# Seven heads' queries and keys and one head's forget gates as four pairs of seven block products ahead of the attention

## The chip, the cores and the metric

One core of one Trainium2 chip runs the whole kernel. TensorE (PE in the profile) multiplies, VectorE (DVE), ScalarE (ACT) and GpSimd (POOL) do the rest, SyncE (SP) issues DMAs, and so do ACT and POOL. The metric is the device time of one execution in microseconds; lower is better.

## The reference

One encoder layer on 1024 tokens of width 1024. The input is RMS-normalised and multiplied by one wide weight matrix; its columns are queries, keys and values of an attention with 8 heads of 64, then forget gates `f`, values `i`, queries `q` and output gates `g` of a gated recurrence (HGRN2) with 4 heads of 128, then two merge gates.

```python
xn = rmsnorm(x, norm1_g[layer])
u = xn @ w_in[layer].astype(f32)
c = np.cumsum([SB_WIDTH, SB_WIDTH, SB_WIDTH, HG_WIDTH, HG_WIDTH, HG_WIDTH, HG_WIDTH, D_MODEL])
q_sb, k_sb, v_sb, f_raw, i_hg, q_hg, g_hg, gate_sb, gate_hg = jnp.split(u, list(c), axis=-1)
...
z = jnp.einsum('bhqd,bhkd->bhqk', qi, k) * scale
mask = kpos[None, :] < qpos[:, None]
log_beta = jax.nn.log_sigmoid(z)
log_rem = jnp.where(mask, log_beta - z, 0.0)
between = lax.cumsum(log_rem, axis=3, reverse=True) - log_rem
w = jnp.where(mask, jnp.exp(log_beta + between), 0.0)
return jnp.einsum('bhqk,bhkd->bhqd', w, v)
...
h = x.astype(f32) + merged @ w_out[layer].astype(f32)
hn = rmsnorm(h, norm2_g[layer])
a = jnp.square(jax.nn.relu(hn @ w_ff1[layer].astype(f32)))
h = h + a @ w_ff2[layer].astype(f32)
```

The two branches are gated and merged, projected, added to the input, and a squared-ReLU MLP and a last RMSNorm follow.

## The kernel before

**Numbers in two parts.** Every matmul operand is split into a high part (ACT copies to the rounded type, `hi_copy`) and a low part (DVE subtracts, `lo_sub`); `hi_lo` does both, and `three` multiplies high by high, high by low and low by high. A block of 128 output columns, 512 tokens and 512 inputs is 12 matmuls of 512 columns.

**Stages.** First x is loaded, normalised and transposed into `xn` (two halves of 512 tokens, each as high and low slots), while head 0's queries and keys (`qk0`) and the first four heads' values (`v0`) are projected. Then comes the attention, then the recurrence (`hg_levels`, `hg_tail`) with the merge gates' products as filling, then the merge, the output projection and the MLP. The merge gates, the output projection and the MLP already use sums of blocks, with seven block products in place of eight.

**Attention.** `items` holds 8 heads times 8 query blocks in the order 7, 0, 6, 1, 5, 2, 4, 3. For each item `scores` (L774 on) multiplies the query block with the keys and lets ACT take the sigmoid into `rm`; `weights` runs the products from right to left as one scan on DVE (L821; two scans for block 7); `turn` transposes the result on PE, ACT subtracts one into `wTh` (L869) and DVE makes `wTl` (L875); `values` multiplies two finished blocks with V, and ACT and DVE add the halves of the result (L903, L904). The loop issues the scores of item i+2, the scan of item i+1 and the turn of item i.

**Order.** A planner orders instructions at compile time by their place in the program and their readiness; on PE two lanes are held in order by hand: "main" (the attention) and "fill" (projections), where a fill block waits for the main block two before it. `Stream` holds fill jobs; each call of `step` issues one piece (six matmuls of 512 columns, or twelve of 256). When a job starts, its weights are split, and `prefetch` splits those of the next job and loads those of the one after. All loads on SP's queue keep the program's order (`load`).

**What fills the attention.** The stream `st` holds qk0 with v0, qk1 to qk3, v1 (the other four heads' values), qk4 to qk7, then f0, q0, i0, g0 of the recurrence, f1, q1, g1 and then raw job 0 of the merge gates. The loop issues 126 steps over 64 items, so that everything up to g0 is done in the attention. `qk_epilogue` writes the keys' high and low parts into one slot (KS, high in partitions 0 to 63, low in 64 to 127) and the queries' into two (QH, QL), and POOL copies each query part into the other 64 partitions by a DMA.

**Storage.** 40 slots of 128 x 1024 floats and 10 halves of 128 x 512 hold nearly all data; raw weights and their two parts have two buffers each (`wpool`).

Of the kernel before, what the change touches and what calls it, by code (L numbers as in the profile page):

```python
# [9 lines left out]
F32 = mybir.dt.float32  # L10
# [29 lines left out]
def kernel(  # L40
# [493 lines left out]
    st = Stream()  # L534
# [158 lines left out]
    def qk_epilogue(h):  # L693
        def ep(ps, half):
            if half == 0:
                qk[h] = tuple(slot(f"{n}{h}", F32R) for n in ("QH", "QL", "KS"))
            QH, QL, KS = qk[h]
            cs = slice(half * 512, (half + 1) * 512)
# [12 lines left out]
    def v_job(quad):  # L711
        unit = v_unit(quad)
        return st.add(
            [unit], lambda: token_steps(f"pjv{quad}", unit, xn, range(NT), v_epilogue(quad))
        )

    def qk_item(h):
        u = cols_unit(f"wqk{h}", [(W_IN, C_Q + h * DHS, DHS), (W_IN, C_K + h * DHS, DHS)])
        return f"pjqk{h}", u, qk_epilogue(h)
# [24 lines left out]
    def first_job():  # L744
# [4 lines left out]
        def body():  # L749
            v_ep = v_epilogue(0)  # L750
            for half, parts in enumerate((((0, 2), (2, 2)), ((0, 4),))):
                ps = bank(f"{name}_{half}")
                for b0, n in parts:
# [4 lines left out]
                    if half == 0 and b0 > 0:  # L758
                        st.prefetch()
# [3 lines left out]
        return st.add([u_qk], body), u_qk, u_v  # L763

    j_first, u_qk0, u_v0 = first_job()
    j_qk = {0: j_first}
    for h in range(1, NHS):
        j_qk[h] = proj_jobs([qk_item(h)], xn)
        if h == 3:
            j_v = v_job(1)  # L770
# [144 lines left out]
    def hg_slot(h, key, half):  # L915
        if half == 0:
# [52 lines left out]

    def hg_jobs(h):  # L970
        for key, c0, ep in (
            ("f", C_F, f_epilogue(h)),
            ("q", C_QH, silu_epilogue(h, "q")),
            ("g", C_GH, silu_epilogue(h, "g")),
        ):
            if key == "g" and h % 2 == 0:
                i_job(h)
            u = cols_unit(f"w{key}{h}", [(W_IN, c0 + h * P, P)])
            j_hg[h] = proj_jobs([(f"pj{key}{h}", u, ep)], xn)

    hg_jobs(0)
# [442 lines left out]

    j_raw = []
    hg_jobs(1)
    j_raw.append(raw_job(0))
    hg_jobs(2)
    j_raw.append(raw_job(1))
    j_raw.append(raw_job(2))  # L1430
    hg_jobs(3)
# [723 lines left out]
    st.advance(4, 1)  # L2155
    u_v0.split()
    norm1((2, 3))
    st.advance(3, 1)
    norm_transpose(xn, 0, 2, 2)
    st.advance(5, 1)  # L2160
    norm1(range(4, NT))
    st.advance(4, 1)
# [4 lines left out]
    st.advance(11, j_qk[0])  # L2167
    first_row()
# [169 lines left out]
```

## Time and profile before

| | |
|---|---|
| median of 3 runs | 1459.29 us (1457.73 to 1460.15) |
| profiled execution | 1460.9 us, span 1458.7 us |
| start to first score | 0 to 50.3 us |
| attention, first score to last value matmul | 50.3 to 322.3 us |
| recurrence and its filling | 322.3 to about 700 us |

The span is the time between the first and last instruction that the profiler saw. A row of stretches gives, after the stretch and its length, each engine's busy time with the number of instructions, then the granted share of the TensorE clock, the DMA engines' busy share and GB/s. A group's row gives line, engine, operation, destination and sources, shapes and count, then busy time, mean ns of one, idle time before it and what ended it. A timeline row gives start and length in us. A row of waits gives total, times and longest, in us.

### The profile page before, as it was taken

To read this page: it belongs to the slowest core of one execution; us is meant where nothing else is said; L and a number is where in the kernel's file an instruction comes from. 1 tells how busy PE (TensorE), PEld (TensorE's weight loads), DVE (VectorE), ACT (ScalarE), POOL (GpSimd) and SP (SyncE) were. 2 spreads that over 40 slices of the span, in tenths; PEclk is the share of its full clock that TensorE was granted. 3 is DMA by queue.
4 is the path that set the end of the run, shared out by engine and by line. 5 is a ranking of instruction groups with operands and counts; after the bars stand their busy time and mean duration, and the time that the engine had idled before them with its cause. 6 is when DMAs were issued, how large, how long until landed. Compare 5 with 4: busy or idle time off the path is not lost. (4 is left out here: it accounts for less than half of the span.)

```text
span 1458.7 us, 19714 instructions
## 1 busy us (share of the span) xinstructions
PE 1438.6 (99%) x7470; PEld 1224.4 (84%) x7470; DVE 1060.9 (73%) x1498; ACT 645.8 (44%) x1068; POOL 164.1 (11%) x306
## 2 busy tenths in 40 slices
PE   9999999999999999999998999999999999999998
PEld 8889888988898888888877888888888888888886
DVE  6576788679747688877756898666666757768765
ACT  7454565542313234433344575444444533523433
POOL 4222232200000012100010210000000000000032
PEclk9999999999999999999999999999999999999999
DMA  7344364311313249655478513444445975676835
GB/s 227 88 120 102 83 117 98 74 36 44 94 30 101 63 133 246 228 176 180 139 211 291 186 62 133 171 152 152 159 159 171 347 266 196 240 275 244 284 103 182
DMA packets 159862, 232.00 MB, mean 159 GB/s; under 512 B 26092, under 2 KB 94232, under 8 KB 159768
## 3 DMA queue, kind: packets, MB, share of 16 engines
q1 hardware_dynamic: 142552, 183.29, 37.4%
q0 software_dynamic: 13472, 40.91, 11.2%
q10 hardware_dynamic: 3744, 6.56, 1.2%
q8 instruction: 59, 0.97, 0.3%
q14 instruction: 35, 0.29, 0.1%
HBM read 166.75 MB, written 63.97 MB: 158 GB/s over the span
## 5 line engine op out<-in xcount | busy, mean ns | idle before, releaser
L821 DVE TENSOR_TENSOR_SCAN rm<-rm,bits 128x512 f32<-128x512 f32 (+6 forms) x72 | 87.2, 1222 | 27.3 <-ACT rm L795 26.9
L154 ACT CAST whid<-w 128x1024 fp32r<-128x1024 f32 x30 | 31.6, 1053 | 154.4 <-PE pm L131 83.7
L131 PE MATMUL pm<-wlod,sh 128*128 128x512 f32 x240 | 93.5, 390 | 0.0
L131 PE MATMUL pm<-whid,sl 128*128 128x512 f32 x240 | 93.4, 389 | 0.0
L131 PE MATMUL pm<-whid,sh 128*128 128x512 f32 x240 | 93.4, 389 | 0.0
L131 PE MATMUL pm<-tl,sh 128*128 128x512 f32 (+1 forms) x210 | 81.3, 387 | 0.0
L131 PE MATMUL pm<-th,sh 128*128 128x512 f32 (+1 forms) x210 | 81.3, 387 | 0.0
L131 PE MATMUL pm<-th,sl 128*128 128x512 f32 (+1 forms) x210 | 81.3, 387 | 0.0
L875 DVE SCALAR_TENSOR_TENSOR wTl<-pw,wTh 128x512 fp32r<-128x512 f32 (+2 forms) x96 | 50.6, 549 | 38.8 <-ACT wTh L869 38.5
L159 DVE TENSOR_TENSOR wlod<-w,whid 128x1024 fp32r<-128x1024 f32 x30 | 36.7, 1222 | 57.0 <-ACT whid L154 57.0
L869 ACT ACTIVATE wTh<-pw,minus_one 128x512 fp32r<-128x512 f32 (+2 forms) x96 | 53.1, 581 | 45.0 <-PE pw L134 43.4
L159 DVE TENSOR_TENSOR sl<-sa,sh 128x1024 fp32r<-128x1024 f32 x56 | 68.1, 1217 | 0.5 <-ACT sh L154 0.5
L1979 POOL TENSOR_SCALAR fss<-fss 128x1 f32<-128x1 f32 x8 | 4.5, 562 | 562.5 <-ACT fsc L1974 562.0
L154 ACT CAST sh<-sa 128x1024 fp32r<-128x1024 f32 x56 | 57.2, 1046 | 6.2 <-DMA sa<-ad 6.2
L131 PEld LDWEIGHTS pm<-wlod,sh 128*128 128x128 f32 x240 | 45.0, 187 | 9.9 <-DVE wlod L159 0.4
L131 PEld LDWEIGHTS pm<-whid,sl 128*128 128x128 f32 x240 | 45.1, 188 | 9.4
L131 PEld LDWEIGHTS pm<-whid,sh 128*128 128x128 f32 x240 | 45.1, 188 | 9.2
L131 PE MATMUL pX<-sql,t1h 128*128 128x512 f32 x128 | 50.1, 391 | 0.1
L131 PE MATMUL pX<-sqh,t1h 128*128 128x512 f32 x128 | 49.9, 390 | 0.1
L131 PE MATMUL pX<-sqh,t1l 128*128 128x512 f32 x128 | 49.8, 389 | 0.0
L795 ACT ACTIVATE rm<-z 128x512 f32<-128x512 f32 (+3 forms) x96 | 43.6, 489 | 8.6 <-PE z L131 7.5
L131 PEld LDWEIGHTS pm<-tl,sh 128*128 128x128 f32 x210 | 39.5, 188 | 8.1
(929 smaller groups left out, 4546.9 us busy)
## 6 DMA issues: line engine op xcount, KB each, us to landing
w<-in_w_ff_dram SPq DMA_DIRECT2D x72, 512.0 KB, 5.4
sa<-ad SPq DMA_DIRECT2D x56, 512.0 KB, 6.6
ad<-a SPq DMA_DIRECT2D x32, 256.0 KB, 4.1
ad<-s SPq DMA_DIRECT2D x16, 512.0 KB, 4.7
tw<-in_w_out_dram POOLq DMA_DIRECT2D x24, 256.0 KB, 4.7
x<-in_x_dram SPq DMA_DIRECT2D x8, 512.0 KB, 8.9
vr<-vrows POOLq DMA_DIRECT2D x16, 256.0 KB, 5.1
xnl<-xnh POOLq DMA_DIRECT2D x8, 512.0 KB, 9.9
```

Source lines behind the costliest of these rows:

```text
L131: return pe(nc.tensor.matmul(*a, **k))
L154: hi_last[0] = after(in_turn("act", nc.scalar.copy(dst, src)), hi_behind[0])
L159: nc.vector.tensor_tensor(out=dst, in0=src, in1=hi.bitcast(F32), op=ALU.subtract),
L795: nc.scalar.activation(rm[:, s0 : s0 + m], z[:, :m], AF.Sigmoid, scale=-0.125)
L821: sc = nc.vector.tensor_tensor_scan(out=rr, data0=rr, data1=bits[:, 1024 - nk + a : 1024 - nk + b][:, ::-1], initial=rm[:, b : b + 1] if i ...
L869: nc.scalar.activation(th[:, 0:n, qs], src, AF.Identity, bias=minus_one),
L875: nc.vector.scalar_tensor_tensor(out=tl[:, 0:n, qs], in0=src, scalar=-1.0, in1=th[:, 0:n, qs].bitcast(F32), op0=ALU.add, op1=ALU.subtract,),
L1979: nc.gpsimd.tensor_scalar(out=ssq, in0=ssq, scalar1=1.0 / D, scalar2=EPS, op0=ALU.mult, op1=ALU.add)
```

## The change

The projections of q and k for heads 1 to 7 and of f0 leave the stream. They become eight blocks of 128 columns in four pairs, (qk1, qk2), (qk3, qk4), (qk5, qk6), (qk7, f0), and each pair is computed ahead of the attention as seven block products (`ProjPair`) in place of eight: both column blocks, both halves of the tokens and both halves of the 1024 inputs give a two by two block product.

- `early_whole` adds the high and low parts of `xn` back together, the first half on POOL, the second on DVE; `early_sums` makes four sums of blocks from them and splits each into two parts. Products 3, 5, 6 and 7 use these, products 1, 2 and 4 use `xn` itself.
- Each pair loads two raw weight blocks, splits the first as it is (`split_plain`, products 1 and 2) and forms sums and differences of both (`split_sums`, products 3 to 7).
- Products 1, 6, 7 and 4 accumulate in bank X with copies by ACT in between; 5 and 3 in Y; 2 in Z; DVE adds the copies (`value`).
- Queries and keys are no longer kept: `qk_store` splits each half and writes both parts to DRAM (POOL's queue), also for head 0; `qk_load` reads a head back by six loads on SP's queue into KS, QH and QL.
- A second stream `front` holds qk0 with v0, and v1. Eight steps of v1 run before the pairs, three in the last pair, two between the first two scores, the rest in the attention.
- `st` now begins with raw job 0 and q0, i0, g0; the loop issues 45 steps over 64 items. In item 2 of a head the next head's q and k are read, in item 3 its values (item 2 before), in item 5 its values are split.

```diff
-    def qk_epilogue(h):
-        def ep(ps, half):
-            if half == 0:
-                qk[h] = tuple(slot(f"{n}{h}", F32R) for n in ("QH", "QL", "KS"))
...
-            hi_copy(KS[0:64, cs], ps[64:128])
-            hi_copy(QH[0:64, cs], ps[0:64])
-            lo_sub(KS[64:128, cs], ps[64:128], KS[0:64, cs])
-            last_lo[0] = lo_sub(QL[0:64, cs], ps[0:64], QH[0:64, cs])
-            for Q in (QH, QL):
-                nc.gpsimd.dma_start(Q[64:128, cs].bitcast(F32), Q[0:64, cs].bitcast(F32))
+    def qk_store(h):
+        def ep(src, half_):
+            cs = slice(half_ * 512, (half_ + 1) * 512)
+            hi, lo = half(f"qkh{h}_{half_}", F32R), half(f"qkl{h}_{half_}", F32R)
+            last_lo[0] = hi_lo(hi, lo, src)
+            for n, t in (("h", hi), ("l", lo)):
+                nc.gpsimd.dma_start(qkd[h, n][:, cs], t.bitcast(F32))
...
+    def qk_load(h):
+        qk[h] = QH, QL, KS = tuple(slot(f"{n}{h}", F32R) for n in ("QH", "QL", "KS"))
+        hi, lo = qkd[h, "h"], qkd[h, "l"]
+        q, k = slice(0, DHS), slice(DHS, P)
+        for t, r, src in (
+            (KS, q, hi[k]), (QH, q, hi[q]), (KS, k, lo[k]), (QH, k, hi[q]), (QL, q, lo[q]),
+            (QL, k, lo[q]),
+        ):
+            load(t[r].bitcast(F32), src)
...
+    def early_whole(half_, engine):
+        for kp in range(KT // 2):
+            h, l = (t.bitcast(F32) for t in xn.t[half_, kp])
+            early[half_, kp // 2, kp % 2] = t = slot(f"xw{half_}{kp}")
+            engine.tensor_tensor(out=t, in0=h, in1=l, op=ALU.add)
...
+        for kp in range(2):
+            tt(w[1, 1, kp], w[1, 0, kp], w[1, 1, kp], ALU.add)
+            tt(w[1, 0, kp], w[0, 0, kp], w[1, 0, kp], ALU.subtract)
+            tt(w[0, 0, kp], w[1, 1, kp], w[0, 0, kp], ALU.subtract)
+            form(6, kp, w[0, 0, kp])
...
+        def split_plain(self):
+            hl = self.wts("a")
+            hi_lo(*hl, self.raw[0])
...
+        def split_sums(self):
...
+            sub_(ra[:, a], rb[:, a], ra[:, a])
+            sub_(rb[:, a], rb[:, b], rb[:, a])
+            self.w[3] = tuple(half(f"w3{n}{self.i}", F32R) for n in "hl")
+            hi_lo(*self.w[3], rb[:, b])
+            sub_(rb[:, b], rb[:, b], ra[:, a])
+            sub_(ra[:, b], ra[:, b], rb[:, b])
+            hl = self.wts("b")
+            hi_lo(*hl, rb)
+            self.w[7], self.w[6] = self.halves_of(hl)
+            hl = tuple(slot(f"w54{n}{self.i}", F32R) for n in "hl")
+            hi_lo(*hl, ra)
...
-    j_raw = []
-    hg_jobs(1)
-    j_raw.append(raw_job(0))
+    j_raw = [raw_job(0)]
+    hg_job(0, "q")
+    hg_job(0, "g")
...
+    early_whole(0, nc.gpsimd)
+    front.advance(4, 1)
     norm_transpose(xn, 1, 0, 4)
...
+    early_whole(1, nc.vector)
+    early_sums()
...
+    front.finish(j_first)
+    front.advance(8, j_v)
+    proj[0].load()
+    proj[0].split_plain()
+    proj[0].m1()
+    proj[0].split_sums()
+    for o, n in zip(proj, proj[1:] + [None]):
+        o.m2()
+        if n:
+            n.load()
+        o.m6()
+        o.m5()
+        if n:
+            n.split_plain()
+        o.m7()
+        if n:
+            n.m1()
+            n.split_sums()
+        else:
+            qk_load(0)
+            v_load(0)
+            front.advance(3, j_v)
+        o.m4()
+        o.m3()
...
-    n_fill = 9 * (j_hg[0] - j_qk[0]) + 18
-    n_first = 3
+    n_fill = 3 + 7 + 2 * 9 + 17
+    n_first = 0
...
-        if ahead < NHS and i % NHS in (2, 5):
+        if ahead < NHS and i % NHS in (2, 3, 5):
             if ahead == NHS // 2:
-                st.finish(j_v)
-            (v_load if i % NHS == 2 else v_split)(ahead)
+                front.finish(j_v)
+            {2: qk_load, 3: v_load, 5: v_split}[i % NHS](ahead)
...
-        upto = (j_hg[2], j_hg[3], j_raw[5], j_sb[1], j_sb[3])[h]
+        upto = (j_hg[2], j_hg[3], j_raw[6], j_sb[1], j_sb[3])[h]
```

More of the change, by code (lines that the diff above doesn't have):

```diff
@@ L758, in body @@
                     if half == 0 and b0 > 0:
-                        st.prefetch()
+                        front.prefetch()
                     tb = 4 * half + b0
                     yield from token_steps("pjv0", u_v, xn, range(tb, tb + n), v_ep, tb == 0)
-        return st.add([u_qk], body), u_qk, u_v
+        return front.add([u_qk], body), u_qk, u_v
     j_first, u_qk0, u_v0 = first_job()
[L766 to L770, printed above, removed]
+    j_v = v_job(1)
@@ L915, in hg_slot @@
     def hg_slot(h, key, half):
-        if half == 0:
+        if (h, key) not in hg:
             hg[h, key] = slot(f"{key}{h}")
```

158 lines of the change are left out of this document (127 added, 31 removed).

## The prediction

> **What bounds the kernel now.** I read the page first (share of each engine), then the stretches of the stage in question, then PE's waits, then single rows for prices.
>
> ```profile
> span 1458.7 us, 19714 instructions
> PE 1438.6 (99%) x7470; PEld 1224.4 (84%) x7470; DVE 1060.9 (73%) x1498; ACT 645.8 (44%) x1068; POOL 164.1 (11%) x306
> ```
>
> ```profile
> core 0: us, PE busy (x) PEld busy (x) DVE busy (x) ACT busy (x) POOL busy (x), PEclk, DMA share, GB/s
> 50.30:322.30 272.00, 267.85 (x1691) 239.78 (x1690) 197.28 (x268) 148.90 (x308) 66.17 (x146) 0.99 0.41 91
> 322.30:700.00 377.70, 377.70 (x2117) 322.53 (x2116) 292.46 (x521) 127.56 (x243) 34.45 (x50) 1.00 0.42 129
> ```
>
> ```profile
> PE po L131 <- DVE wTl L875: 3.0, 3, 1.6
> PE po L131 <- ACT wTh L869: 0.6, 1, 0.6
> PE z L131 <- ACT rm L795: 0.5, 1, 0.5
> ```
>
> PE is busy in 99% of the span. That share alone says little, as matmuls overlap; but the waits of PE in the attention (first score matmul at 50.3 us, last value matmul at 322.3) come to 4.1 us of 272.0. So TensorE sets the pace there and in the 377.7 us of the recurrence behind it. DVE has 197.28 us of 272.0, 73%. The reader should keep both: matmuls removed are worth their full time only as long as DVE stays below PE.
>
> **What the change removes.** Block prices:
>
> ```profile
> 884.94 2.72 PE pW L131 x12
> 887.66 2.72 PE pY L131 x12
> ...
> 40.61 0.28 PE L131 MATMUL pjv<-wv0h,xnl 128*128 128x256 f32 x1
> 40.73 0.28 PE L131 MATMUL pjv<-wv0h,xnh 128*128 128x256 f32 x1
> ```
>
> Twelve matmuls of 512 columns (one block of K 512 by 512 tokens in three passes) take 2.72 us; a matmul of 256 columns starts 0.12 us after the one before. Seven q/k projections and f0 are 8 x 4 = 32 blocks, 87.0 us. Four pairs of seven products are 28 blocks, 76.2 us. Saved: 4 x 2.72 = **10.9 us** of PE. The count of matmuls is fixed by the code, so that the saving of work fails to come is no case.
>
> **What it moves.** Nothing of the 76.2 us lies beside the attention any more; it runs ahead, with 11 of the 16 steps of v1 (1.44 us each, 15.8 us). Into the attention comes raw job 0 (36 matmuls, 3 x 2.72 = 8.2 us) out of the recurrence. Two small pieces change sides, by the rows of the attention's last 10 us and first 3 us:
>
> ```profile
> L131 PE MATMUL pjf<-xnl,wf1h 128*128 128x512 f32 x4 | 1.6, 390 | 0.0
> ...
> L131 PE MATMUL pjv<-wv0h,xnl 128*128 128x256 f32 x5 | 1.4, 281 | 0.0
> ```
>
> One pass of three is shown: 12 matmuls of f1 (2.7 us) go back to the recurrence, and 15 of v0 (1.8 us) that ran behind the first scores run ahead. The attention by PE is then 272.0 - 87.0 - 15.8 - 2.7 - 1.8 + 8.2 = **172.9 us**. Were PE the bound throughout, the span would be 1458.7 - 10.9 = 1447.8.
>
> **DVE in the new attention.** The rows, all of the attention:
>
> ```profile
> L821 DVE TENSOR_TENSOR_SCAN rm<-rm,bits 128x512 f32<-128x512 f32 (+6 forms) x72 | 87.2, 1222 | 27.3 <-ACT rm L795 26.9
> L875 DVE SCALAR_TENSOR_TENSOR wTl<-pw,wTh 128x512 fp32r<-128x512 f32 (+2 forms) x96 | 50.6, 549 | 38.8 <-ACT wTh L869 38.5
> L904 DVE TENSOR_TENSOR osb<-po,ot 64x256 f32<-64x256 f32 x30 | 12.6, 419 | 7.4 <-ACT ot L903 7.1
> L159 DVE TENSOR_TENSOR KS<-pjqk,KS 64x512 fp32r<-64x512 f32 x14 | 9.7, 695 | 2.9 <-ACT QH L154 2.7
> L159 DVE TENSOR_TENSOR QL<-pjqk,QH 64x512 fp32r<-64x512 f32 x14 | 9.5, 682 | 0.2
> L159 DVE TENSOR_TENSOR V<-vr,V 128x512 fp32r<-128x512 f32 x8 | 5.5, 684 | 0.7 <-ACT V L154 0.7
> L685 DVE TENSOR_TENSOR vr<-vr 128x512 f32<-128x512 f32 x8 | 5.4, 670 | 0.8 <-DMA vr<-vrows 0.8
> L159 DVE TENSOR_TENSOR wi0l<-wi0r,wi0h 128x1024 fp32r<-128x1024 f32 x2 | 2.3, 1208 | 0.0
> L167 DVE TENSOR_TENSOR g<-pjg,g 128x512 f32<-128x512 f32 x2 | 1.4, 692 | 0.6 <-ACT g L963 0.6
> ...
> L154 ACT CAST KS<-pjqk 64x512 fp32r<-64x512 f32 x14 | 8.2, 583 | 2.4 <-PE pjqk L131 2.1
> L154 ACT CAST QH<-pjqk 64x512 fp32r<-64x512 f32 x14 | 8.1, 580 | 0.2
> ```
>
> The KS and QL rows (19.2 us) go, and the weight splits of the seven projections. What stays: scans 87.2, wTl 50.6, osb 32 x 0.42 = 13.4, seven V splits 7 x 1.35 = 9.5, six low parts of weights (raw 0, q0, two of i0, g0, f1) 6 x 1.21 = 7.3, raw job 0's other work (one 1024 difference, three 512 operations) 1.2 + 3 x 0.68 = 3.2, the q0 and g0 products 4 x 0.69 = 2.8. Sum **174.0 us**, against 172.9 for PE. The bound passes to DVE, or both stand level. ACT is no bound: 148.90 us less the 28 KS and QH copies (16.3 us) and the weight casts of the projections.
>
> How tightly can DVE run? The rows that bound it:
>
> ```profile
> 50.45 0.40 PE L131 MATMUL z<-KS,QH 128*128 128x512 f32 x1
> 52.24 2.96 DVE L821 TENSOR_TENSOR_SCAN rm<-rm,bits 128x512 f32<-128x512 f32 x3 [7.04 <-ACT rm L795]
> ...
> 228.20 2.01 DVE L821 TENSOR_TENSOR_SCAN rm<-rm,bits 128x896 f32<-128x896 f32 x1
> 230.13 0.66 DVE L875 SCALAR_TENSOR_TENSOR wTl<-pw,wTh 128x512 fp32r<-128x512 f32 x1
> ...
> 104.00:124.00 20.00, 17.74 (x126) 16.82 (x125) 18.63 (x25) 12.09 (x26) 4.76 (x12) 0.91 0.49 110
> 320.00:360.00 40.00, 40.00 (x236) 34.12 (x236) 38.64 (x87) 10.92 (x18) 0.00 (x0) 1.00 0.19 54
> ```
>
> A scan of 2.01 us is followed 1.93 us after its start: ready instructions overlap by 0.07 to 0.08 us, so some 228 of them need 174 - 16 = 158 us at the least. And where DVE was behind, it was busy 18.63 of 20 us in the attention (after a stall of ACT at 104) and 38.64 of 40 in the recurrence: 93 and 97%, the rest goes to waits on ACT. With 1.8 us from the first score (50.45) to the first scan (52.24) and 0.6 us behind the last operation (an estimate: two matmul starts and an ACT copy), the ends are 158 / 0.97 + 2.4 = 165 (hidden under PE's 173) and 174 / 0.93 + 2.4 = 189.5. I take the rows laid end to end, overlap and waits cancelling as in the stretch at 104: 174 + 2.4 = **176 us**, 3.1 more than PE needs. In this stage PE idles for those 3.1 us and nothing later makes them up, since PE is full from 322.3 on.
>
> **The front.** The forms of x and the weight sums have to be ready in time.
>
> ```profile
> 34.80 0.50 PE L131 MATMUL pjqk<-xnh,wqk0whi 128*128 128x512 f32 x1
> ...
> 33.56 4.68 DVE L335 SCALAR_TENSOR_TENSOR xnl<-xnt,prm,xnh 128x512 fp32r<-128x512 f32 x7
> ...
> L1991 POOL TENSOR_TENSOR hb<-hb,gf 128x512 f32<-128x512 f32 x1 | 1.3, 1283 | 0.0
> ```
>
> The second half of qk0 starts on PE at 34.80; DVE is free from 38.2. It must do 20 operations of 1024 columns (four whole inputs, eight sums, eight low parts) of 1.21 us each (the wi0l row), 24.2 us, one more for the plain weights and 4.6 us of weight sums before product 6: 30.0 us, or 28 with overlap. PE comes to product 6 of pair 0 after the second half of qk0 (5.5), four tokens of v0 and four of v1 (2 x 11.5) and two products (5.4): 34 us after 34.8, at 68.8. That is 30.6 us of room: level. POOL's four additions (2 x 1.28 each by the 512 row, 10.3 in all) can start before that, once the first half of x is there. Afterwards each pair asks about 12 us of DVE (seven sums and low parts 6.7, three values, four low parts of the stores) per 7 x 2.72 = 19.0 us of PE, and its accumulators are copied while another bank's product runs, so no product waits. The 32 stores of q and k replace the 32 copies of Q on POOL's queue one for one. I take **2 us** lost in the front; ends 0 and 8 (POOL's part not overlapped). V split 0 and the ramp to the first scan lie beside two v1 steps (2.9 us).
>
> **Reading back.** Per head six loads of 256 KB on SP's queue, behind and ahead of the weight loads.
>
> ```profile
> wqk4r<-in_w_in_dram SPq DMA_DIRECT2D x2, 256.0 KB, 7.2
> vr<-vrows POOLq DMA_DIRECT2D x16, 256.0 KB, 5.1
> ...
> SPq L139 <- DVE wqk6l L159: 51.8, 1, 51.8
> ```
>
> They are issued at item 2 and needed by the scores issued at item 6: four items, 176 / 64 x 4 = 11 us, against six issues and a landing of 5 to 7 us. DMA share is 0.41. I cost this at nothing: hidden by the four items. If that cover goes, scores, ACT, scan and PE all stand.
>
> **Sum.** 1458.7 - 10.9 + 3.1 + 2.0 = 1452.9 of span. The profiled execution took 1460.9 with that span of 1458.7, 2.2 us around it; the median shown is 1459.3, 1.6 below it. I carry the difference of -5.8 over to the median: **1453.5 us**.
>
> **Rivals.** (a) DVE keeps up: the waits of 27 and 39 us in its rows are PE's doing and vanish, PE stays the bound. 1458.7 - 10.9 + 0 to 2: median 1448.4 to 1450.4, less if the 4.1 us of waits go too. For it: 97% at 320 to 360 beside a full PE. Against: 174 over 172.9.
>
> (b) Slower: **waits on ACT in a DVE-bound attention**. With no projection left to put between, a scan waits for its sigmoid and wTl for wTh. At 93% of the full rows the attention is 189.5 long: 1447.8 + 16.6 + 2 = 1466.4, median 1467; it is slower than before once the attention exceeds 172.9 + 10.9 - 2 = 181.8 us, that is with DVE's full rows filling less than 97% of it. Middle of this case: 1462.
>
> (c) Slower: **the read-back is late**. SP's queue is in order; if a weight load stands in it for its buffer (one stood 51.8 us), q and k stand behind it. Five us at each of seven head switches is 35 us: 1490. Long gaps also slow PE:
>
> ```profile
> 107.00:108.00 1.00, 0.08 (x1) 0.08 (x1) 1.00 (x3) 1.00 (x2) 0.15 (x1) 0.75 0.28 57
> 108.00:109.00 1.00, 1.00 (x5) 1.00 (x6) 1.00 (x2) 0.96 (x3) 0.38 (x1) 0.50 0.13 29
> 110.00:111.00 1.00, 1.00 (x7) 1.00 (x6) 0.81 (x2) 0.00 (x0) 0.86 (x4) 0.55 0.51 111
> ```
>
> After some 2 us of idle PE the granted clock fell to 0.50; the three microseconds shown lost 0.25 + 0.50 + 0.45 = 1.2 us, 8 us over seven switches. The Trainium skill (TensorE: Matmul & The Clock Gate, What's actually happening) says the clock halves after an idle window of about 3.4 us; the trace shows it after a shorter wait.
>
> (d) **The front is late**: POOL's four additions and DVE's two-input ones do not run side by side, DVE loses up to 10.3 us of room that is already level: 8 us more, median 1461.5. No row shows a large addition on POOL beside DVE. The Trainium skill (GPSIMD Engine Reference, Key points) says the two share SBUF interfaces and contend when DVE has two SBUF inputs.
>
> **Chances.** (a) 0.22; forecast, 1450.4 to 1458, 0.43, its own range; (b) 0.20; (c) 0.07; (d) 0.08. About 0.2% (2.9 us) is what a measurement of this kernel can tell from no change. Below 1456.4: all of (a) and 0.33 of the forecast, 0.55. Above 1462.2: 0.10 of (b), all of (c), 0.03 of (d), 0.20. The rest, 0.25. The range 1447 to 1466 leaves out (c) and the far ends of (a) and (b).
>
> **What would show it.** PE with 48 fewer matmuls; a front from about 52 to 144 us with PE full; an attention of about 176 us with DVE over 90% and PE some 95%; from its end to the end of the kernel some 1131 us (1136.4 + 2.7 - 8.2). It is wrong if the attention's DVE stays under 90%, if PE waits at product 6 of pair 0, or if scores wait for a DMA at head switches.

## The result: slower by 3 %

The changed kernel took 1502.91 us (median of four runs, 1500.56 to 1505.72) against 1459.72 us for the kernel before, measured beside it. The ratio is 1.030, with a 95 % interval of 1.0275 to 1.0319. The prediction was 1453.5 us, with a range of 1447 to 1466: wrong in sign, and by 49 us. The profiled execution took 1505.72 us with a span of 1504.0 us; it is the slowest of the four, so stage lengths from it may be some 3 us too long.

The head of the page after (span, then busy time, share and instructions of each engine):

```profile
span 1504.0 us, 19848 instructions
PE 1444.2 (96%) x7422; PEld 1227.2 (82%) x7422; DVE 1101.0 (73%) x1538; ACT 658.6 (44%) x1080; POOL 171.9 (11%) x310
```

The 48 matmuls are gone (7470 to 7422), and yet PE is busy longer, in a longer span, at a smaller share: it stands more, and some of its matmuls run slowly. Where, the view by stretches tells. I cut at three points that are the same work in both kernels: the first score matmul, the first state product of the recurrence (`sd`), the end. First the kernel before, then the changed one (start and end, length, busy time of each engine, granted clock, DMA share, GB/s):

```profile
0.00:50.45 50.45, 47.46 (x349) 45.51 (x349) 28.87 (x55) 30.54 (x60) 17.53 (x39) 1.00 0.65 189
50.45:326.42 275.97, 271.82 (x1708) 243.03 (x1707) 201.28 (x282) 150.45 (x312) 66.17 (x146) 0.99 0.41 90
326.42:1458.70 1132.28, 1119.29 (x5417) 935.83 (x5415) 830.72 (x1162) 464.79 (x698) 80.37 (x121) 1.00 0.52 174
```

```profile
0.00:156.15 156.15, 144.57 (x840) 128.80 (x841) 99.94 (x133) 71.30 (x117) 45.42 (x76) 0.97 0.49 148
156.15:375.71 219.56, 185.79 (x1193) 166.38 (x1191) 173.50 (x244) 122.17 (x269) 48.14 (x115) 0.92 0.61 136
375.71:1504.00 1128.29, 1113.79 (x5393) 931.99 (x5391) 827.60 (x1162) 465.16 (x696) 78.31 (x120) 1.00 0.52 173
```

The prediction's span of 1452.9 us, cut at the same points, is 144 for the front, 1132.28 + 2.7 - 8.2 = 1126.8 for the last stretch, and the 182.1 between them:

| stage | predicted | measured | difference |
|---|---|---|---|
| front, to the first score | 144 | 156.15 | +12.2 |
| attention, to the first state product | 182.1 | 219.56 | +37.5 |
| rest | 1126.8 | 1128.29 | +1.5 |

The rest came out as forecast. The attention holds the largest part. DVE's work in it is 173.5 us; up to the last value matmul, where the forecast's stage ends, it is 170.6 against the forecast's 174.0. But it is spread over 219.6 us: DVE is busy for 79 % of the stretch, PE for 85 % and at a clock of 0.92. Neither engine is busy throughout; both wait. PE's largest waits from 20 to 375 us (total, times, longest, in us):

```profile
PE pw L134 <- DVE rm L972: 11.9, 2, 11.2
PE po L131 <- DVE wTl L1026: 9.9, 13, 3.3
PE xnt L134 <- DVE x L640: 7.5, 2, 5.4
PE pga L131 <- ACT wga0whi L154: 4.9, 1, 4.9
PE z L131 <- DMA QH<-qkh: 2.0, 1, 2.0
PE pgq L131 <- ACT wga0t L154: 1.8, 1, 1.8
```

These six are 38 us, 30.5 of them in the attention, where all waits before came to 4.1. Most of the rest of the loss goes with the clock of 0.92: the same 1193 matmuls are busy for 185.79 us here and for 176.55 in e14 below, at 0.98. Four places make up most of the list. The timeline shows each (start and length in us; in brackets the idle time before, and what ended it).

**Place 1, the front at 27 us.** VectorE scales x for the second half of the tokens while GpSimd begins to add the parts of the first half (first VectorE, then GpSimd, then TensorE):

```profile
25.84 0.76 DVE L640 TENSOR_SCALAR x<-x,n_y 128x1024 f32<-128x1024 f32 x1 [1.62 <-POOL n_y L253]
27.31 2.90 DVE L640 TENSOR_SCALAR x<-x,n_y 128x1024 f32<-128x1024 f32 x1 [0.71 <-POOL n_y L253]
33.25 0.75 DVE L640 TENSOR_SCALAR x<-x,n_y 128x1024 f32<-128x1024 f32 x1 [3.04 <-POOL n_y L253]
37.01 2.82 DVE L640 TENSOR_SCALAR x<-x,n_y 128x1024 f32<-128x1024 f32 x1 [3.01 <-POOL n_y L253]
```

```profile
27.25 2.41 POOL L785 TENSOR_TENSOR xw<-xnh,xnl 128x1024 f32<-128x1024 f32 x1
29.74 0.51 POOL L249 TENSOR_SCALAR n_ss<-n_ss 128x1 f32<-128x1 f32 x1
30.34 2.37 POOL L785 TENSOR_TENSOR xw<-xnh,xnl 128x1024 f32<-128x1024 f32 x1
32.67 0.55 POOL L253 TENSOR_TENSOR n_y<-n_ss,expo 128x1 f32<-128x1 f32 x1
```

```profile
34.06 0.41 PE L134 MATMUL xnt<-ident,x 128*128 128x128 f32 x1 [2.04 <-DVE x L640]
39.89 5.58 PE L134 MATMUL xnt<-ident,x 128*128 128x128 f32 x29 [5.42 <-DVE x L640]
```

Two things happen. The scaling that starts at 27.31, just after an addition, takes 2.90 us in place of 0.76: it ends 0.55 us after the addition. The last scaling is caught in the same way, by the fourth addition (36.94 to 39.28 us). And the norm's own small GpSimd steps (`n_ss`, `n_y`) queue behind additions, so that the last two scalings start 3.04 and 3.01 us late. TensorE stands 2.04 us for the third scaling and 5.42 for the last, and then runs slowly, as the granted clock says (the number before the last two, stretches of 5.0 and 5.4 us):

```profile
35.00:40.00 5.00, 0.11 (x1) 0.12 (x2) 2.99 (x2) 0.00 (x0) 4.95 (x4) 0.50 0.00 2
40.00:45.40 5.40, 5.40 (x30) 5.23 (x30) 5.40 (x8) 4.22 (x7) 1.26 (x2) 0.59 0.65 201
```

**Place 2, the start of the attention.** GpSimd's queue, then VectorE, then TensorE:

```profile
153.13 0.54 POOL L705 DMA_DIRECT2D qkh<-qkh  x1 [13.24 <-ACT qkh L154]
153.85 0.54 POOL L705 DMA_DIRECT2D qkl<-qkl  x1 [0.18 <-issue]
154.39 1.80 POOL L676 DMA_DIRECT2D vr<-vrows  x2
```

```profile
167.22 0.69 DVE L685 TENSOR_TENSOR vr<-vr 128x512 f32<-128x512 f32 x1 [9.84 <-DMA vr<-vrows]
167.83 0.42 DVE L972 TENSOR_TENSOR_SCAN rm<-rm,bits 128x128 f32<-128x128 f32 x1
```

```profile
170.86 1.11 PE L134 MATMUL pw<-ident,rm 128*128 128x128 f32 x4 [11.15 <-DVE rm L972]
191.41 0.79 PE L131 MATMUL pga<-xnh,wga0whi 128*128 128x512 f32 x1 [4.86 <-ACT wga0whi L154]
```

The load of head 0's values stands in GpSimd's queue behind two stores, the first of which waited 13.24 us for ScalarE. It is issued at 154.39 and lands at 167.2. VectorE's subtraction waits for it, the first scan stands behind the subtraction, and TensorE waits 11.15 us for the scan.

**Place 3** is the last row: the attention's first filling job asks for its weights when it starts, and TensorE stands 4.86 us for them. **Place 4** is the value loads of the later heads: VectorE's waits from 160 to 345 us name them, two waits of 3.4 us together beside the 9.84 above, and each holds up the scans queued behind:

```profile
DVE vr L685 <- DMA vr<-vrows: 13.2, 3, 9.8
```

### The profile page after: what moved, and what is told of

It reads as the page before. It is cut to its first block, busy times and chain, and to the rows that moved or that the text cites. A ratio compares the mean times of both kernels' runs of the same rounds, so it can differ in the third digit from the quotient of the medians.

```text
span 1504.0 us, 19848 instructions
## 1 busy us (share of the span) xinstructions
PE 1444.2 (96%) x7422; PEld 1227.2 (82%) x7422; DVE 1101.0 (73%) x1538; ACT 658.6 (44%) x1080; POOL 171.9 (11%) x310
## 3 DMA queue, kind: packets, MB, share of 16 engines
q0 software_dynamic: 14496, 45.10, 10.9%
## 5 line engine op out<-in xcount | busy, mean ns | idle before, releaser
L1020 ACT ACTIVATE wTh<-pw,minus_one 128x128 fp32r<-128x128 f32 (+3 forms) x96 | 54.2, 587 | 27.4 <-PE pw L134 25.0
L134 PE MATMUL pw<-ident,rm 128*128 128x128 f32 x288 | 46.4, 286 | 11.9 <-DVE rm L972 11.9
L1026 DVE SCALAR_TENSOR_TENSOR wTl<-pw,wTh 128x128 fp32r<-128x128 f32 (+3 forms) x96 | 50.6, 546 | 9.7 <-ACT wTh L1020 9.3
L134 PEld LDWEIGHTS pw<-ident,rm 128*128 128x128 f32 x288 | 36.8, 148 | 16.8 <-DVE rm L972 12.6
L131 PE MATMUL po<-wTh,V 128*128 128x256 f32 x160 | 45.5, 312 | 5.1 <-DVE wTl L1026 3.3
```

The lines of the kernel that those rows point to most:

```text
L131: return pe(nc.tensor.matmul(*a, **k))
L134: return pe(nc.tensor.transpose(dst, src, ident))
L1020: nc.scalar.activation(th[:, 0:n, qs], src, AF.Identity, bias=minus_one),
L1026: nc.vector.scalar_tensor_tensor(out=tl[:, 0:n, qs], in0=src, scalar=-1.0, in1=th[:, 0:n, qs].bitcast(F32), op0=ALU.add, op1=ALU.subtract,),
```

## The experiments

The first eleven kernels have one run each. Kernels with four to thirteen runs ranged over 3.6 to 9.1 us, so a difference of 3 us between single runs settles nothing by its total; for those I go by stages and by single waits. The last four have several runs each, with intervals. First the three suspects that stand alone.

**e1, GpSimd's additions behind the norm's own steps**

```diff
-            engine.tensor_tensor(out=t, in0=h, in1=l, op=ALU.add)
+            after(engine.tensor_tensor(out=t, in0=h, in1=l, op=ALU.add),
+                  last_power[0] if engine is nc.gpsimd else None)
```

> The four additions of the first half's whole input stay on POOL but stand behind the last norm's power. Theory A (the front lost its time because tokens 4 to 7 waited for POOL's small steps between additions of 2.4 us, and DVE's scaling ran 2.8 in place of 0.75 us beside them): the last input transpose, 45 us after the start in the changed kernel, comes back to about 35, the first score from 156 to about 146, total 1502.9 - 10 = 1493. Rival (early sums or wider loads hold the start): the first score stays at 154 or later, total above 1500.

Measured: 1504.77 us, no gain. The last transpose came at 35.6 us instead of 45.2, as the theory has it, but the first score only at 153.9 instead of 156.15, as the rival has it. The additions had moved into VectorE's next work: one scaling took 2.87 us and two splits of weights 6.07, as in e4 below.

**e2, head 0's values sooner**

```diff
         o.m6()
+        if not n:
+            v_load(0)
...
             qk_load(0)
-            v_load(0)
```

> Only the loads of head 0's values are moved, to just behind product 6 of the last pair. Theory B (the first scan stood behind V's subtraction on DVE and the sigmoid behind V's cast on ACT, and the load had been queued on POOL behind the last stores): the 11.3 us gap of PE behind the first scores shrinks to 3 us or less, total about 1493. Rival (DVE is the bound of the attention, as forecast): DVE's work is the same, what is won at the start is lost later, total within 3 us of 1503.

Measured: 1492.47 us, 10.4 less than the changed kernel's median, as the theory has it. The wait of 11.15 us is gone, and the attention is 209.0 us long instead of 219.6. Place 2 costs what it shows.

**e3, the first filling job's weights sooner**

```diff
             n.split_sums()
+            if n is proj[3]:
+                raw_units[0].load()
         else:
+            raw_units[0].split()
```

> Only raw job 0's weights are moved: loaded behind the last pair's own weight sums and split behind its product 7, where DVE is idle. Theory C (PE stood 5 us at raw job 0's first matmul and 2 us at its third product, because its cast was late on ACT, and then ran at half clock): these waits and the half clock behind them go, total 1503 - 7 to 10 = 1493 to 1496. Rival (DVE-bound attention): PE's idle time only moves; beyond the 3.6 us of DVE work that leaves the attention nothing is won, 1499 to 1503.

Measured: 1499.51 us, 3.4 less than the median: by its total the rival. The attention is 214.2 us long, 5.4 less, of which 3.4 us are VectorE's work that left it (173.5 to 170.1). TensorE's wait of 4.86 us is gone, the one of 1.8 us for the third product is not. What place 3 costs in the total is not settled by this run.

**e4, all three**

> The three edits together. If A, B and C add up: 1503 - 10 - 10 - 8 = about 1475, an attention of some 190 us, still 14 over the forecast. Rival (DVE-bound): A only, and the attention stays over 205 us, total about 1490.

Measured: 1485.07 us, 17.8 less than the median, with an attention of 200.8 us: between the theory and the rival. Spans add up (1504.0 to 1503.1, 1490.8 and 1497.8 with one edit each, 1483.3 with all). What e1's edit did is seen here, VectorE first and GpSimd second:

```profile
29.68 2.86 DVE L640 TENSOR_SCALAR x<-x,n_y 128x1024 f32<-128x1024 f32 x1 [0.72 <-POOL n_y L253]
33.06 6.07 DVE L159 TENSOR_TENSOR wv1l<-wv1r,wv1h 128x1024 fp32r<-128x1024 f32 x2
```

```profile
29.61 11.74 POOL L786 TENSOR_TENSOR xw<-xnh,xnl 128x1024 f32<-128x1024 f32 x4
```

One scaling still takes 2.86 us, and two splits of weights take 6.07 us where 2.4 is usual (2.35 in e6 below). So the additions hold VectorE up here too, and not only where the norm's steps are queued; and they are held up themselves, with 11.74 us for four where e7 below has 9.25.

**e5 and e6, the additions behind VectorE's last split, and the values' loads sooner.** e5 is e4 with the additions ordered behind the last split of the second value block and issued after the transposes:

```diff
-                last_power[0] if engine is nc.gpsimd else None,
+                last_split[0] if engine is nc.gpsimd else None,
```

> As the run with all three edits (e4, 1485.07 us), but GpSimd's four additions of the first half wait for VectorE's last split of the second value block, so that they lie beside VectorE's reads of PSUM and no longer beside its scalings of x and its two weight splits. In e4 one scaling of x took 2.86 us instead of 0.75 and the two splits 6.07 us instead of 2.4, and TensorE stood from 35.98 to 39.85 us and ran at the half clock until about 45. Theory (a GpSimd addition and a VectorE operation that reads SBUF at two places do not run side by side): the x takes 0.75, the splits 2.4, the first score comes 4 to 7 us sooner (at 147 to 150 instead of 153.8), total 1478 to 1481. Rival (the additions only need 9 to 12 us of GpSimd somewhere, and VectorE's chain of sums ahead of product 6 is late by what is gained): the first score stays at 152 to 154, total 1483 to 1486.

e6 is e5 with the loads of the next head's values moved from item 3 to item 1:

```diff
-        if ahead < NHS and i % NHS in (2, 3, 5):
+        if ahead < NHS and i % NHS in (1, 2, 5):
...
-            {2: qk_load, 3: v_load, 5: v_split}[i % NHS](ahead)
+            {1: v_load, 2: qk_load, 5: v_split}[i % NHS](ahead)
```

> As e5, with the load of the next head's values two items sooner: at item 1 of a head, ahead of the queries and keys (item 2), instead of item 3; the split stays at item 5. In e4 VectorE waited 3.2 us at 201.5 for such a load, with the additions of the reflections behind it, and TensorE 3.78 us for them. Theory (the loads' lateness is what thins the attention): VectorE's waits for vr go to nothing and the time falls by 3 to 8 us against e5. Rival (the attention is thin because VectorE and TensorE are nearly equal in work and wait for each other in turn): the waits for vr go, but others fill the gap: 0 to 3 us against e5.

Measured: 1490.98 us for e5, more than e4 and outside both of its ranges; 1472.05 us for e6. The two have the same front in the code, and yet the first score came at 156.8 us in e5 and at 150.3 in e6. The splits tell why: `after` gives the planner an order but the engines no wait, and fractions of a microsecond decided which engine was held up. (By the profile the split that was held in e7 starts 0.58 us ahead of the first addition; what decides in so close a case is not shown.) The two splits of e6; then one of the two of e7 (below), and GpSimd's additions beside it. e5 has 12.07 us for its two:

```profile
31.02 2.35 DVE L160 TENSOR_TENSOR wv1l<-wv1r,wv1h 128x1024 fp32r<-128x1024 f32 x2
```

```profile
32.42 10.92 DVE L160 TENSOR_TENSOR wv1l<-wv1r,wv1h 128x1024 fp32r<-128x1024 f32 x1
```

```profile
33.00 9.25 POOL L788 TENSOR_TENSOR xw<-xnh,xnl 128x1024 f32<-128x1024 f32 x4
```

A single split waited for all four additions: it ends at 43.34 us, 1.1 us after the last of them. Apart from that front, the attention went from 204.1 us (e5) to 191.6 (e6): 12.4 us for the values' loads, more than the 3 to 8 that I expected.

**e11, the values' loads alone**, e6's edit on the changed kernel:

> The changed kernel (1502.91 us) with one edit alone: the load of the next head's values at item 1 of a head, ahead of the queries and keys, instead of item 3. Between e5 and e6 this edit came with a front that was 6.5 us shorter by chance, and the attention from first score to the first state product fell from 204.1 to 191.6 us. Theory (late values cost the attention 9 to 12 us): from first score to first state product 207 to 211 us instead of 219.6; total 1490 to 1495. Rival (most of the gain was that of the front): total 1498 to 1503.

Measured: 1500.67 us, 2.2 less than the median, as the rival has it. The attention became 9.8 us shorter (209.7), as the theory has it, but the stretch behind it was 5.1 us longer than in the changed kernel (1133.4 against 1128.3). Most of that lies in one place, 243 us behind the first state product: there TensorE waits 2.82 us for VectorE (`pp`; 1.72 us in the changed kernel), and the 10 us behind the wait ran at a granted clock of 0.70 (first row) instead of 1.00 (second row, the changed kernel):

```profile
608.35:618.35 10.00, 10.00 (x47) 8.37 (x48) 6.63 (x15) 2.49 (x4) 1.13 (x2) 0.70 1.02 322
617.46:627.46 10.00, 9.99 (x65) 8.58 (x66) 9.00 (x18) 4.04 (x6) 1.13 (x2) 1.00 1.04 321
```

By the last product for `pys`, just behind this place, 3.6 of the 5.1 us are lost. e1 shows the same wait with 2.3 us and a clock of 0.80 to 0.86 behind it. So this part of the loss is not special to e11's edit. The effect on the attention is shown twice, that on the total is not settled by this run.

**e7 and e8, one pair's work back into the attention.** e7 is e6 with three pairs in front; head 7's queries and keys and the first forget gates are plain products again, as filling work. TensorE has 2.7 us more to do.

```diff
+    name7, u_qk7, ep7 = qk_item(NHS - 1)
+    proj_jobs([(name7, u_qk7, ep7)], xn)
+    hg_job(0, "f")
     j_raw = [raw_job(0)]
...
-    proj = [ProjPair(i, *blocks[2 * i : 2 * i + 2]) for i in range(4)]
+    proj = [ProjPair(i, *blocks[2 * i : 2 * i + 2]) for i in range(3)]
...
-    n_fill = 3 + 7 + 2 * 9 + 17
+    n_fill = 3 + 7 + 4 * 9 + 17
```

> As e6, with three pairs in front instead of four: the queries and keys of head 7 and the forget gates of head 0 are plain block products again (8 of 2.72 us for 7), run as filling work in the attention, 18 steps more there. TensorE's own work grows by 2.7 us. Theory (the attention was left with too little TensorE work that waits for nothing: TensorE 160 us of work in about 193): the front gets 19 us shorter, the attention grows by only 3 to 10 us, since 21.8 us of filling work goes into the gaps; total 10 to 16 us less than e6. Rival (the waits in the attention are late loads and weights, whatever the filling work): the attention grows by 19 to 22 us, total as e6 or up to 3 us more.

Measured: 1472.38 us, as e6; but its front had the split of 10.92 us, and e6's had not. The attention grew from 191.6 to 204.75 us, 13.1 for 21.8 us of work, between the theory and the rival. e8 makes the additions really wait, by a small GpSimd operation that reads the split's last column:

```diff
+    gate = small.tile([P, 1], F32, tag="gate", name="gate")
+    nc.gpsimd.tensor_scalar(out=gate, in0=last_split[0][:, 1023:1024].bitcast(F32),
+                            scalar1=1.0, scalar2=None, op0=ALU.mult)
     early_whole(0, nc.gpsimd)
```

> As e7 (three pairs in front, 1472.38 us), with one small GpSimd operation ahead of its four additions that reads the last column of VectorE's last split, so that the additions really wait for it: in e5 to e7 the edit only gave an order, and in e7 the additions began at 32.7 us while a split of VectorE's was waiting, which then took 10.92 us (12.07 for the two in e5, 2.35 in e6, where the split had started first). Theory: both splits take 1.2 us each, the transposed half is ready 8 to 10 us sooner, the first score comes at 128 to 130 instead of 137.2, and the total is 1462 to 1466. Rival (VectorE's sums ahead of product 6 take it back): 1468 to 1472.

Measured: 1467.57 us. The first score came at 130.2 us, 7.0 sooner than in e7, but the total fell by 4.8 only, between the theory and the rival. Part went to a wait that was hidden behind the late front until then, at product 6 of the first pair (TensorE, then ScalarE):

```profile
72.74 0.79 PE L131 MATMUL ppX<-efh,whib 128*128 128x512 f32 x1 [3.54 <-ACT pu L891]
```

```profile
71.16 1.05 ACT L155 CAST whib<-wp0b 128x1024 fp32r<-128x1024 f32 x1 [5.41 <-DVE wp0b L853]
```

ScalarE's copy of the first product (`pu`) stands behind the cast of the summed weights, and that cast waited 5.41 us for VectorE's sums.

**e9 and e10, two attempts on e8.** e9 puts a second pair's work into the attention (first diff, and 18 filling steps more); e10 moves the 32 transfers that build the output weights' sums behind the first two heads (second diff).

```diff
-    proj_jobs([(name7, u_qk7, ep7)], xn)
+    plain = [qk_item(h) for h in range(5, NHS)]
+    for item in plain:
+        proj_jobs([item], xn)
...
-    proj = [ProjPair(i, *blocks[2 * i : 2 * i + 2]) for i in range(3)]
+    proj = [ProjPair(i, *blocks[2 * i : 2 * i + 2]) for i in range(2)]
```

```diff
-        if i % 2 == 1:
+        if i >= 16 and i % 3:
             next(wsums, None)
```

> As e8, with only the two pairs of heads 1 to 4 in front, and heads 5, 6, 7 and the first forget gates as plain products in the attention (TensorE's own work 2.7 us more than e8, the front 19 us shorter, 21.8 us more of filling work in the attention). Theory (with one pair's work moved, e7 against e6, 21.8 us of filling work made the attention only 13.1 us longer; the gaps left are some 16 us): the attention grows by 17 to 21 us, total between 2 us less and 3 us more than e8. Rival (the waits shrink again by as much as the first time): 5 to 8 us less than e8.

> As e8, with the 32 GpSimd transfers that build the sums of the output weights moved: none in the attention's first two heads, then two of every three items instead of every second one. Theory (these transfers lengthen the landing of the weights, the queries and the keys just where the first filling jobs start: in e7 TensorE waited 3.1 us at 178.9 for the cast of weights that took 12.3 us to land): waits for loads in the first 40 us of the attention go, 2 to 4 us less than e8. Rival (the loads are hidden anyway, or the later heads pay): within 1.5 us of e8.

Measured: 1468.01 us for e9, as e8 and as its theory has it, with two new waits of 2.5 us each for head 6's weights. 1465.55 us for e10, 2.0 less than e8, too little for one run to tell from none; TensorE's wait for the forget gates' weights stayed at 3.1 us, so those transfers alone did not make it.

**e12, the two waits that were left above 2 us**: eleven value steps ahead of the pairs and none in the last pair, and a prefetch when the first filling job starts.

```diff
-    st, front = Stream(), Stream()
+    st, front = Stream(eager=True), Stream()
...
-    front.advance(8, j_v)
+    front.advance(11, j_v)
...
-            front.advance(3, j_v)
```

> As e10 (1465.55 us), with two edits for the two waits of TensorE that are left above 2 us: the three value steps that stood in the last pair go ahead of the first pair (11 steps there instead of 8), so that ScalarE's copy of the first product, which stands behind the cast of the summed weights, is not late (TensorE waited 3.07 us at 69.0 and ran slow until about 73); and the attention's first filling job asks for the next job's weights when it starts, as all later jobs do (TensorE waited 3.11 us at 171.9 for the cast of the forget gates' weights). Theory (these two waits cost themselves and 1 to 2 us of half clock each): 7 to 9 us less than e10, total 1456 to 1459, no difference from the kernel before. Rival (at the end of the front the steps covered the first values' split, and the ramp opens again by what is gained): 1461 to 1465.

Measured: 1461.83 us, ratio 1.0019 (1.0005 to 1.0032). Both waits are gone, but the time is the rival's, and so is the reason: TensorE now waited 2.4 us for a copy in the last pair, which stood behind head 0's late values. The queries' lower parts also came 1.8 us late at 293 us.

**e13, e14 and e15: every load sooner, with three, four and two pairs in front.** e13 is e12 with the values asked for at item 0 of a head, the queries and keys at item 1, head 0's values ahead of the last pair; e14 is e13 with four pairs, as in the changed kernel, and e15 is e13 with two, by e9's edit:

```diff
-        if not n:
-            v_load(0)
...
                 u_qk7.load()
+                v_load(0)
...
-            {1: v_load, 2: qk_load, 5: v_split}[i % NHS](ahead)
+            {0: v_load, 1: qk_load, 5: v_split}[i % NHS](ahead)
```

> As e12 (1461.83 us, ratio to the kernel before 1.0019), with every read-back one item sooner (the next head's values at item 0, its queries and keys at item 1) and the first head's values asked for ahead of the last pair. In e12 TensorE waited 2.38 us at 119.3, because VectorE and ScalarE waited for the first values (landed at 120.2) with the last pair's copies queued behind, and 1.79 us at 293.5 for the queries' lower parts. Theory (these two are what is left of the change's own waits, each with 1 to 2 us of half clock): 5 to 8 us less than e12: 1454 to 1457, 0.2 to 0.4 % faster than the kernel before. Rival (loads a stage earlier only move the contention among the transfers): 1460 to 1463.

> As e13, but with all four pairs in front as in the changed kernel: the change whole, with loads, additions and first filling jobs moved. TensorE has 2.7 us less work than in e13, and 21.8 us less of filling work in the attention. Theory (with all loads in time the attention still needs the filling work, since VectorE and TensorE are near to equal there: e6 against e8, four pairs against three with the front undisturbed in both, was 4.5 us slower): 2 to 6 us more than e13. Rival (the thinness was late loads alone): 2 to 3 us less than e13.

> As e13, but with two pairs in front (heads 1 to 4); heads 5, 6, 7 and the first forget gates are plain products in the attention. TensorE has 2.7 us more work than in e13, and 21.8 us more of filling work there. Theory (filling work moved from the front into the attention is worth what it fills: from four pairs to three 8.6 us; e13 shows only 4 to 6 us of waits between the first score and the first state product that filling work could take): 0 to 3 us less than e13, 1458.5 to 1462, no difference from the kernel before. Rival (the gaps shrink again by as much): 1453 to 1457, faster than both kernels.

| kernel | pairs in front | median | ratio to before (95 %) | front | attention | rest |
|---|---|---|---|---|---|---|
| after | 4 | 1502.91 | 1.0297 (1.0275 to 1.0319) | 156.15 | 219.56 | 1128.29 |
| e14 | 4 | 1470.34 | 1.0082 (1.0065 to 1.0099) | 146.82 | 192.54 | 1128.64 |
| e13 | 3 | 1461.72 | 1.0020 (1.0010 to 1.0031) | 125.50 | 204.57 | 1130.03 |
| e15 | 2 | 1457.27 | 0.9981 (0.9968 to 0.9995) | 106.64 | 215.60 | 1128.06 |

e13 is not faster than e12: the rival held, and TensorE's waits for queries and keys in e13 come to 3.3 us where e12 had 2.0. e14, the whole change with these loads and additions moved, is still 0.8 % slower than the kernel before, and 8.6 us slower than e13, more than the 2 to 6 of its theory. The attention's stretch of e14, of e13 and of e15:

```profile
146.82:339.36 192.54, 176.55 (x1193) 158.96 (x1192) 169.09 (x240) 121.42 (x268) 47.89 (x115) 0.98 0.61 148
```

```profile
125.50:330.07 204.57, 197.09 (x1299) 177.47 (x1298) 175.75 (x250) 126.89 (x274) 50.97 (x121) 0.98 0.65 157
```

```profile
106.64:322.24 215.60, 214.82 (x1396) 193.06 (x1394) 181.16 (x254) 130.43 (x279) 55.46 (x129) 1.00 0.65 164
```

PE's share of the stage goes from 92 % over 96 % to 99.6 %. Each time 21.8 us of plain products enter the stage, it grows by 12.0 and 11.0 us; the rest of the work lies in gaps that were there. (The profiled run of e15 is 5.3 us faster than its median, so the 11.0 may be too small by as much.) What PE waited for in e14, 20 to 375 us:

```profile
PE pw L134 <- DVE rm L974: 6.8, 6, 3.2
PE po L131 <- DVE wTl L1028: 5.4, 6, 1.4
PE pgq L131 <- ACT wga0t L155: 2.4, 1, 2.4
PE z L131 <- DMA QL<-qkl: 0.8, 1, 0.8
```

DMA is hardly in the list any more. But for the 2.4 us for raw job 0's weights, what is left is the attention's own chain: TensorE for VectorE's scans and low parts. VectorE in turn waited for ScalarE (two rows of its groups in e14, 150 to 370 us; idle time and its releaser at the end), and ScalarE for TensorE (from 146.82 to 339.36 us 31.8 us for the transposes `pw` and 18.8 for the values `po`):

```profile
L974 DVE TENSOR_TENSOR_SCAN rm<-rm,bits 128x512 f32<-128x512 f32 (+6 forms) x72 | 87.3, 1221 | 9.6 <-ACT rm L948 8.8 <-issue 0.5
L1028 DVE SCALAR_TENSOR_TENSOR wTl<-pw,wTh 128x512 fp32r<-128x512 f32 (+2 forms) x96 | 50.1, 545 | 10.8 <-ACT wTh L1022 8.6 <-POOL wTl L1005 1.4 <-issue 0.2
```

e15 keeps half of the saving (5.5 us less TensorE work than before) and is the only version that came out ahead of the kernel before, by 0.2 %, with an interval that just leaves out no change. Its ten runs go from 1451.91 to 1461.01 us, and the profiled one (1451.98) is among its fastest. By its expectation 1457.27 lies between theory (from 1458.5) and rival (to 1457), nearer to the rival.

## Why the prediction was wrong, point by point

**The saving of 10.9 us was right.** 48 matmuls are gone, and from 50 to 150 us the products ran without a gap. The rest of the kernel behind the attention took 1128.3 us against 1126.8 forecast.

**DVE's work was right, its density was not.** This step fails even with the loads in time, and makes the sign wrong by itself (1453.5 + 10.4 is above 1459.7): "How tightly can DVE run?" chose 176 us from rows laid end to end, with two stretches in which DVE was behind (93 and 97 %) as evidence. Both were stretches in which nearly everything that DVE needed lay ready: its waits come to 1.1 of the 20 us and 1.2 of the 40. The first began when DVE had stood 5.63 us and its work had piled up, and in the 20 us behind it DVE was busy for 52 % (the kernel before):

```profile
104.11 1.76 DVE L821 TENSOR_TENSOR_SCAN rm<-rm,bits 128x768 f32<-128x768 f32 x1 [5.63 <-ACT rm L795]
124.00:144.00 20.00, 20.00 (x166) 19.83 (x165) 10.42 (x15) 8.89 (x20) 4.99 (x10) 1.00 0.33 89
```

In the new attention PE and DVE have nearly the same work and each needs the other's results through ACT, so that neither can run far ahead. With the loads in time (e14) DVE is still busy for only 88 % of the stage (169.09 of 192.54 us), below the 90 % that the prediction named as a sign of being wrong. The stage is 10.4 us longer than the 182.1 predicted, and TensorE's gaps close as filling work comes back (e13, e15). That is rival (b): it gave 1467 at its far end, with DVE at 93 %, and e14 took 1470.34. The deciding number was there to be formed: with 172.9 us for PE and 174.0 for DVE, neither engine had time to spare for a wait.

**"V split 0 and the ramp lie beside two v1 steps" was wrong.** I counted the split and the ramp, not the load ahead of them. It stands on GpSimd's queue behind the last stores of the pairs, which I had costed as replacing the copies "one for one": 11.15 us (e2: 10.4 of total).

**"Reading back" was right for queries and keys, wrong for values.** Scores waited 2.8 us for QH and QL where the sum had nothing, so rival (c), with its 35 us, did not come. But the change also moves the values' load from item 2 to item 3, and shortens the items. Of 176 us over 64 items, two items are 5.5 us, against a landing of 5.1 us in the profile before, and of 9.0 in the changed kernel (median from issue to landing at the end of the row):

```profile
vr<-vrows POOLq DMA_DIRECT2D x16, 256.0 KB, 9.0
```

That cover was all but gone by the rows I had quoted; I worked it out for the queries and keys alone. e6 and e11 put the late values at 10 to 12 us of attention.

**The first filling job's weights** were not in the sum at all: the stream's first job has no one ahead of it that loads for it. 4.86 us of wait, 3.4 of total in the one run of e3.

**The front: rival (d), and a larger size.** I took 2 us, with 8 as the end if additions on GpSimd and VectorE's operations do not run side by side. The scalings and splits above did not, and the front was 12.2 us late. The price is not only VectorE's lost time: the norm's steps queue behind the additions too, TensorE stands 7.5 us, and 29 transposes then take 5.58 us at a granted clock of 0.59. The first operation caught was a scaling, with one large input, and not one of the two-input sums that rival (d) named. The Trainium skill (SBUF — State Buffer, Who interferes with whom) calls the pair of ports that the two engines share an exclusive lock, held by whoever issues first for the whole instruction; the scaling of 2.90 us beside an addition of 2.41 agrees. The "level" room at product 6 was right to 3.5 us: in the changed kernel PE did not wait there, and once the front was on time (e8) it waited 3.54 us, for VectorE's sums.

**In sum**, of the 51.1 us between the predicted span and the measured one, 36.0 went when loads, additions and first weights were moved, with the edits of e10 and e12 (1504.0 to e14's 1468.0), and 15.1 stayed: 10.4 in the attention's density, 2.8 in the front, 1.8 behind. By single runs the four places give 10.4 (e2), 3.4 (e3), 12.4 (e6 against e5, in the attention) and 7.0 (e8 against e7, in the front), 33.2 together. In the attention, 27.0 of the 37.5 us went with the lateness; 4.4 us of VectorE's work (173.50 to 169.09) left the stage by the same edits, so not all of the 27.0 is waiting. What the 2.8 and the 1.8 us consist of was not tried. No rival alone gave 1503 us: (b) and (d) came together, with the values' loads and the first job's weights, two terms that the sum had at nothing.

## What to carry to other kernels

Work that waits for nothing is worth more in a stage where two engines feed each other than in a stage of its own: taking it out shortens the stage only until the second engine's work is as long, and from there the gaps open. Before moving it, form the sums of both engines with it gone, and keep some difference between them; here half of the change came out 0.2 % ahead, and the whole of it 0.8 % behind with the loads in time. And when a stage shrinks, every load that was hidden "by so many items" has to be counted again in the new, shorter items, the first one and those on other queues too.

## What the runs showed of the hardware

A VectorE scaling or split that meets a GpSimd addition of 128 x 1024 numbers does not just slow down, it is held until the addition is over, and not always by one addition only: in e7 a split of 1.2 us took 10.92 us, through four GpSimd additions one after another (9.25 us). In e4 the two engines took turns instead, 6.07 us for the two splits and 11.74 for the four additions; what decides between the two is not shown. In e6, with the splits ahead, the same pair took 2.35 us. An operation on 128 x 4 numbers was caught likewise (3.95 us, 0.16 in the kernel before), while one that reads an input from PSUM (`xnl`) ran through at its pace beside the same additions, 0.67 us each. VectorE, then GpSimd, in e8:

```profile
33.01 4.03 DVE L336 SCALAR_TENSOR_TENSOR xnl<-xnt,prm,xnh 128x512 fp32r<-128x512 f32 x6
...
39.77 3.95 DVE L227 TENSOR_TENSOR lmx<-prm 128x4 f32<-128x4 f32 x1
```

```profile
34.21 9.48 POOL L787 TENSOR_TENSOR xw<-xnh,xnl 128x1024 f32<-128x1024 f32 x4
```
